# Two transformer blocks on one Trainium2 core: elementwise work moved off GpSimd, one PSUM division, zero-padded GLA queries, means taken earlier

## The chip, the core and the metric

The program runs on one core of a Trainium2 chip, in one launch. A core has a matrix engine (TensorE, called PE in the rows; its weight loads are listed apart as PEld), a vector engine (DVE), a scalar engine (ACT), GpSimd (POOL) and SyncE (SP), which issues the transfers from memory. TensorE reads operands from the on-chip SBUF and writes into PSUM, which has eight banks of 128 partitions by 512 floats. DVE and ACT read PSUM and SBUF; GpSimd works here on SBUF alone. The metric is device microseconds (us) for one execution.

## The reference, cut to what matters

Two blocks run one after the other on 512 tokens of width 1024 (the first with 16 extra "meta" tokens). All of it is in fp32.

```
first_block:   h += 0.5 * swiglu(rmsnorm(h))
               q,k,v,u,g_attn,g_ssm = split(rmsnorm(h) @ w_in)
               attn = sliding_window_attention(q,k,v)     # 16 heads of 64, blocks of 128, sink softmax
               y    = gelu(s5_ssm(u))                     # diagonal complex scan over time
               h   += (sigmoid(g_attn)*attn + sigmoid(g_ssm)*glu(y)) @ w_out
               h   += 0.5 * swiglu(rmsnorm(h)) ; return rmsnorm(h)
second_block, two layers i:
               m = mla_mixer(x) if i == 0 else gla_mixer(x)   # MLA: 16 heads with rope; GLA below
               x = layer_norm(sqrt(2)*x + m)                  # ln1
               x = layer_norm(sqrt(2)*x + conv_ffn(x))        # ln2
               x = x + sigmoid(x @ w_gate + b) * (p[i] @ w_proj)
gla_mixer, 4 heads, chunks n of 64 tokens:
               state = state * decay[n] + k_dec[n]^T v[n] ;  o[n] = q[n] @ state
               o = normalise(o) per head ; o * silu(r) @ w_o
```

## The kernel before, in words

Activations lie transposed: the residual is eight tiles `h` (`hr` without the meta tokens) of 128 features by the tokens. A projection (`proj`, `mm3`, L176) takes each fp32 weight tile of 128x1024, which `fetch` (L138) splits into a high part on ACT (`whi`, L86) and a low part on DVE (`wlo`, L66), and each operand likewise (`zh`, `zl`, or `mh`, `ml`), and adds the three products hi*hi, lo*hi, hi*lo in one PSUM bank. `nat` (L192) does the same with tokens on the output's partitions, 256 columns at a time. Both use the fp32r type, where a matmul is one record in the trace; a plain fp32 matmul is two records ("x2" in a row is one matmul).

The stages: swiglu of the first block; a projection stage; attention of the first block with four quarters of the state-space model woven in (`scores1` L717, `turn1`, `values1`, `ssm_quarter` L540); gates and output (`m3`), second swiglu; the MLA layer (`project`, `scores`, `turn`, `values`, `output`, L1171 to L1260); its two layer norms and convolution FFN (`conv_ffn` L981); the GLA layer (`recur` L1369); its two norms and FFN. A scheduler orders each engine's instructions when the program is built, from its own estimates; each engine then runs its queue strictly in that order, so an instruction that waits holds all that is queued behind it.

What the change touches:

- `pss` (L98) gives a PSUM bank under a tag, `banks` (L102) closes the pool of banks and opens another. Before, the division changes between b=6, s=2 (FFNs) and others for attention, MLA (L1262) and GLA (L1424).
- `sumsq` (L228) adds squares for an rms norm on GpSimd, except the last add.
- `ssm_quarter`: `t0` to `t3` (tiles `sq`, 128x528) are rotated by the tables `ct`, `st` (tile `tab`), scanned along time (L580, L581) and rotated back; of the eight full-width elementwise operations three are on DVE and five on GpSimd. Their results are the operands of the matmuls at L592 and L593.
- `scores1`: for each pair of heads the second head's probabilities (`sc`, times `dn` in tile `at`) are scaled on GpSimd in one operation.
- `Norm` (L886) is a layer norm. `centre` (L894) takes a mean over the first feature tile with a matmul by `oness` (L897) and subtracts it from all eight tiles before squares are summed. `put(k, m)` (L901) adds the mixer's or FFN's output tile `m` to `x`, and sums `x` (`ad`) and its square (`acc`, squares `nq`), the latter on GpSimd for k<5. `sums` (L924) reduces both on TensorE (L928), `factors` makes rsqrt, `bcast` (L240) spreads it by transposes (L244), `apply` (L942) scales, shifts and splits the eight tiles for the next projections.
- For ln1 of layer 0 the mean is taken in `mixer` (L1288), after the third group of MLA's output projection and ahead of the fourth; for ln1 of layer 1 in `put(0)`, with the first output tile.
- `rotate` (L1105) is rope: `x` is read from PSUM by one DVE multiplication over 128 partitions and four over 32.
- `recur` (L1369) runs GLA's recurrence. Per chunk one matmul (L1377) makes the update, DVE updates the state `S` (L83), and L1388 multiplies the queries `gq` of 64 tokens with the state: a stationary operand of 64 columns, into one half of a bank's partitions.

## Time and profile before

| | |
|---|---|
| three runs | 2620.64 us median (2620.52 to 2621.66) |
| profiled execution | 2621.09 us, span of the core 2619.3 us |
| TensorE busy | 2580.6 us, 99% of the span |
| TensorE's mean granted clock | 0.995 of full (2.4 GHz) |
| DVE, ACT, POOL busy | 1589.7, 962.0, 232.2 us |

A row of the timeline gives start, duration, engine, source line, operation, output<-inputs, shape and count, and in brackets the idle time just before it with what ended it. A matmul's modelled duration overlaps the next one's, so what one costs is read from start to start.

### The profile page before, as it was taken

How to read it: one execution, taken by the hardware profiler on the slowest of the kernel's cores; microseconds unless marked ns; L12 is line 12 of the kernel's file. 1: busy time of each engine (PE TensorE's matmuls, PEld its weight loads, DVE VectorE, ACT ScalarE, POOL GpSimd, SP SyncE). 2: the span in 40 equal slices, each digit the busy share in tenths (PEclk: the TensorE clock that was granted, in tenths of full speed). 3: DMA queues.
4: the chain of work that ended last, by engine and by line, in shares of the span. 5: the costliest groups of instructions: out<-in, count | busy, mean ns of one | idle time of the engine just before them, and what ended most of it. 6: DMA issues, size and time to landing. Idle time of an engine off the chain costs nothing.

```text
span 2619.3 us, 35036 instructions
## 1 busy us (share of the span) xinstructions
PE 2580.6 (99%) x13918; PEld 2188.3 (84%) x13918; DVE 1589.7 (61%) x2794; ACT 962.0 (37%) x1490; POOL 232.2 (9%) x190
## 2 busy tenths in 40 slices
PE   8999999999999999999999999999999999999999
PEld 8999999766888888887888878888878778888887
DVE  7985444685557544468776775555663356755556
ACT  4222223344333222234444454333353233433333
POOL 1000002231010000010000110000300011100030
PEclk9999999999999999999999999999999999999999
DMA  5443324332333333322112223333232222333332
GB/s 173 132 137 108 97 89 132 103 86 68 102 100 93 98 97 98 98 90 69 53 57 69 66 79 105 97 97 97 80 99 61 76 66 64 121 98 97 97 96 73
DMA packets 87749, 243.32 MB, mean 93 GB/s; under 512 B 20081, under 2 KB 26097, under 8 KB 87458
## 3 DMA queue, kind: packets, MB, share of 16 engines
q1 hardware_dynamic: 87586, 241.08, 30.2%
q8 instruction: 110, 1.80, 0.3%
q14 instruction: 53, 0.43, 0.1%
HBM read 229.11 MB, written 11.93 MB: 92 GB/s over the span
## 4 chain that ended last, share of the span: by engine, by line
PE 93%; DVE 4%; issue 1%; ACT 1%; DMA 0%; SPq 0%; POOL 0%; DVEq 0%; POOLq 0%; ACTq 0%
PE ps_b L176 62%; PE mm L176 16%; PE ps_b L192 6%; PE ps_o L1252 1%; PE ps_q L1224 1%; PE ps_o L1388 1%; PE ps_t L1240 1%; PE ps_u L1377 1%; DVE wlo L66 0%; PE ps_o L782 0%; DVE h L66 0%; DVE sq L66 0%; PE ps_q L1222 0%; PE ps_q L728 0%; PE ps_q L1223 0%
## 5 line engine op out<-in xcount | busy, mean ns | idle before, releaser
L86 ACT ACTIVATE whi<-raw 128x1024 fp32r<-128x1024 f32 (+2 forms) x418 | 432.6, 1038 | 1016.1 <-PE ps_b L176 664.1
L66 DVE TENSOR_TENSOR wlo<-raw,whi 128x1024 fp32r<-128x1024 f32 (+2 forms) x418 | 516.3, 1237 | 332.4 <-ACT whi L86 329.7
L176 PE MATMUL ps_b<-zh,whi 128*128 128x512 f32 (+1 forms) x1656 | 649.5, 393 | 6.9 <-ACT zh L86 2.4
L176 PE MATMUL ps_b<-zh,wlo 128*128 128x512 f32 (+1 forms) x1656 | 643.1, 389 | 0.0
L176 PE MATMUL ps_b<-zl,whi 128*128 128x512 f32 (+1 forms) x1656 | 638.8, 389 | 0.0
L176 PEld LDWEIGHTS ps_b<-zh,whi 128*128 128x128 f32 (+1 forms) x1656 | 310.7, 188 | 78.5 <-ACT zh L86 4.1
L176 PEld LDWEIGHTS ps_b<-zl,whi 128*128 128x128 f32 (+1 forms) x1656 | 310.8, 188 | 67.7 <-issue 2.6
L176 PEld LDWEIGHTS ps_b<-zh,wlo 128*128 128x128 f32 (+1 forms) x1656 | 310.7, 188 | 65.3 <-issue 0.8
L176 PE MATMUL ps_b<-mh,wlo 128*128 128x512 f32 x528 | 206.2, 391 | 0.0
L176 PE MATMUL ps_b<-ml,whi 128*128 128x512 f32 x528 | 205.4, 389 | 0.0
L176 PE MATMUL ps_b<-mh,whi 128*128 128x512 f32 x528 | 205.4, 389 | 0.0
L176 PE MATMUL mm<-zh,whi 128*128 128x264 f32 x800 | 163.1, 285 | 5.7 <-ACT whi L86 5.7
L176 PE MATMUL mm<-zl,whi 128*128 128x264 f32 x800 | 163.3, 285 | 1.7 <-DVE zl L83 1.7
L176 PE MATMUL mm<-zh,wlo 128*128 128x264 f32 x800 | 162.4, 284 | 0.0
L83 DVE SCALAR_TENSOR_TENSOR cv<-ps_b,vec,cv 128x511 f32<-128x511 f32 (+1 forms) x176 | 130.4, 745 | 15.1 <-ACT cv L86 13.7
L66 DVE TENSOR_TENSOR h<-h,ps_b 128x512 f32<-128x512 f32 x109 | 74.7, 686 | 97.5 <-PE ps_b L176 97.2
L176 PEld LDWEIGHTS mm<-zh,whi 128*128 128x128 f32 x800 | 125.0, 190 | 5.8 <-ACT whi L86 5.7
L176 PEld LDWEIGHTS mm<-zl,whi 128*128 128x128 f32 x800 | 125.1, 190 | 2.4 <-DVE zl L83 2.2
L176 PEld LDWEIGHTS mm<-zh,wlo 128*128 128x128 f32 x800 | 124.9, 190 | 0.0
L66 POOL TENSOR_TENSOR acc<-acc,sq 128x512 f32<-128x512 f32 (+1 forms) x26 | 39.2, 1507 | 937.3 <-ACT sq L86 899.2
L176 PEld LDWEIGHTS ps_b<-mh,whi 128*128 128x128 f32 x528 | 99.1, 188 | 21.1 <-issue 0.5
L176 PEld LDWEIGHTS ps_b<-mh,wlo 128*128 128x128 f32 x528 | 99.1, 188 | 21.0 <-issue 0.5
(426 smaller groups left out, 4015.1 us busy)
## 6 DMA issues: line engine op xcount, KB each, us to landing
raw<-in_ffn_w_dram SPq DMA_DIRECT2D x130, 512.0 KB, 3.5
raw<-in_w_up_dram SPq DMA_DIRECT2D x88, 512.0 KB, 3.7
raw<-in_w_down_dram SPq DMA_DIRECT2D x44, 512.0 KB, 3.6
raw<-in_w_in_dram SPq DMA_DIRECT2D x32, 512.0 KB, 3.6
raw<-in_mla_o_dram SPq DMA_DIRECT2D x16, 512.0 KB, 3.6
raw<-in_ple_g_dram SPq DMA_DIRECT2D x16, 512.0 KB, 3.7
raw<-in_glu_dram SPq DMA_DIRECT2D x8, 512.0 KB, 3.6
raw<-in_w_out_dram SPq DMA_DIRECT2D x8, 512.0 KB, 3.5
```

The lines of the kernel that those rows point to most:

```text
L66: return (e or V).tensor_tensor(o, a, b, op=op)
L83: return V.scalar_tensor_tensor(o, a, s, b, op0=op0, op1=op1)
L86: return SC.activation(o, a, f, **kw)
L176: last["pe"] = PE.matmul(o[:, i, :c1 - c0], lhs, x[k][r][:, c0:c1], start=(k == 0 and j == 0), stop=(k == kt - 1 and j == 2))
L192: PE.matmul(o[:m, :n], x[k][a][:, t0:t0 + m], w[b][:, kk_ * c + m0:kk_ * c + m0 + n], start=(k == 0 and i == 0), stop=(k == kt - 1 and i = ...
L1224: PE.matmul(p[:, :N], d["q"][e][:, bs], d["k"][e][:, :N], start=False, stop=True)
L1240: PE.transpose(pt[:, kt * P:(kt + 1) * P], sc[:, kt * P:(kt + 1) * P], ident)
L1252: PE.matmul(po[:, b * P:(b + 1) * P], vt[:, kt, e * P:(e + 1) * P], pT[:, kt * P:(kt + 1) * P], start=(kt == 0), stop=(kt == b))
L1377: PE.matmul(pu[c][:, :256], ek[b][rows, hc], vt[hh][rows, b])
L1388: PE.matmul(po[hh][-1][64 * c:64 * c + 64, (b % 2) * 256:(b % 2) * 256 + 256], qt[hh][:, n * 64:(n + 1) * 64], s_)
```

## The change

Six edits stand in one diff. One PSUM division (b, q and t with two banks, o and s with one) is kept from the end of attention on; `pss` takes the tags b, q, t in turn where b was asked for, and s, o for s; in MLA the tags are taken by name, and in GLA u means q, and o means o, s, t in turn. In the state-space quarters, in `sumsq` (except one call) and in `Norm`, operations that were on GpSimd are on DVE. The second head's scaling in `scores1` is four ACT operations. `centre` is a function of its own: for ln1 it is called during the third group of MLA's output (`gi == 2`) and during the second head of GLA's recurrence (`hh == 1`), and `put` only adds. In `rotate` ACT copies the swapped quarters out of PSUM and DVE works on 128 partitions. GLA's queries stand in a tile with zeros in the other chunk's 64 columns, so that L1388 (L1395 after) has 128 stationary columns and the two chunks add into all 128 partitions.

```diff
@@ -96,6 +96,10 @@
     def pss(tag="b"):
+
+        if tag in turns:
+            turns[tag].append(turns[tag].pop(0))
+            tag = turns[tag][-1]
         tag = tag if tag in psp["tags"] else "b" if "b" in psp["tags"] else "s"
@@ -108,6 +112,8 @@
     woff = {}
+    turns = {}
+    wide = dict(b=["b", "q", "t"], s=["s", "o"])
     zw, aw = 640, T1
@@ -225,7 +231,7 @@
-    def sumsq(tiles):
+    def sumsq(tiles, e=None):
         acc = zp.tile([P, aw], F32, name="acc")
@@ -234,7 +240,7 @@
                 act(sq[:, :n], t, AF.Square)
-                add(acc[:, :n], acc[:, :n], sq[:, :n], None if k == len(tiles) - 1 else GP)
+                add(acc[:, :n], acc[:, :n], sq[:, :n], None if k == len(tiles) - 1 else e)
         return acc[:, :n]
@@ -574,17 +580,17 @@
             mul(t3[:, sl], re, st[:, sl])
-        add(t0, t0, t1, GP)
-        sub(t2, t2, t3, GP)
+        add(t0, t0, t1)
+        sub(t2, t2, t3)
         fl = lambda t: t.rearrange("p a m -> p (a m)")
...
         mul(t0, t1, ct)
-        mul(t2, t1, st, GP)
+        mul(t2, t1, st)
         mul(t1, t3, st)
-        mul(t3, t3, ct, GP)
+        mul(t3, t3, ct)
         sub(t0, t0, t1)
-        add(t2, t2, t3, GP)
+        add(t2, t2, t3)
         py = pss()
@@ -744,7 +750,11 @@
                     mul(mt[:, :, 32 * s_:32 * s_ + NM], t[:, :, :NM], dn.unsqueeze(2).to_broadcast([P, 4, NM]))
-                    mul(t[:, :, NM:W], t[:, :, NM:W], dn.unsqueeze(2).to_broadcast([P, 4, W - NM]), GP if s_ else None)
+                    if s_:
+                        for i in range(4):
+                            act(t[:, i, NM:W], t[:, i, NM:W], AF.Copy, scale=dn[:, i:i + 1])
+                    else:
+                        mul(t[:, :, NM:W], t[:, :, NM:W], dn.unsqueeze(2).to_broadcast([P, 4, W - NM]))
                 live[u] = sc, mt
@@ -800,7 +810,8 @@
                     values1(units[ui - 1])
-        banks(b=6, s=2)
+        banks(b=2, q=2, t=2, o=1, s=1)
+        turns.update(wide)
         with tc.tile_pool(name="m3", bufs=2) as gp_:
@@ -883,43 +894,32 @@
+    def centre(x, a=1.0):
+
+        pc = pss("s")
+        PE.matmul(pc, oness, x)
+        c = zp.tile([P, aw], F32, name="R")[:, :S]
+        act(c, pc, AF.Copy, scale=a)
+        return c
+
     class Norm:
...
-        def __init__(self, pool, xs, a):
-            self.p, self.xs, self.a = pool, xs, a
+        def __init__(self, pool, xs):
+            self.p, self.xs = pool, xs
             self.aq = zp.tile([P, aw], F32, name="acc")[:, :S]
...
-        def centre(self):
...
         def put(self, k, m):
             x = self.xs[k]
+            add(x, x, m)
             if k == 0:
-                if self.a == 1.0:
-                    add(x, x, m)
-                else:
-                    stt(x, x, self.a, m, ALU.mult, ALU.add)
-                    self.centre()
-                    sub(x, x, self.c)
-                    for t in self.xs[3:]:
-                        stt(t, t, self.a, self.c, ALU.mult, ALU.subtract)
                 act(self.aq, x, AF.Square)
                 return
-            if self.a != 1.0 and k < 3:
-                stt(x, x, self.a, m, ALU.mult, ALU.add)
-                sub(x, x, self.c)
-            else:
-                add(x, x, m)
             sq = self.p.tile([P, S], F32, name="nq", bufs=3)
...
             add(self.ad, self.ad if k > 1 else self.xs[0], x)
-            add(self.aq, self.aq, sq, GP if k < 5 else None)
+            add(self.aq, self.aq, sq)
@@ -951,7 +951,7 @@
                 else:
-                    ts(xs[k], xs[k], gk, bk, e=GP)
+                    ts(xs[k], xs[k], gk, bk)
                 return chain(lambda: sub(z[k][1], xs[k], z[k][0].bitcast(F32)), prev)
@@ -978,7 +978,7 @@
-    def conv_ffn(li, xs, a, mixer):
+    def conv_ffn(li, xs, mixer):
@@ -1011,10 +1011,10 @@
-            norm = Norm(ph, xs, a)
+            norm = Norm(ph, xs)
             mixer(norm)
             z = close(norm, "ln1", "w_up")
-            norm = Norm(ph, xs, 1.0)
+            norm = Norm(ph, xs)
@@ -1038,6 +1038,7 @@
             def down(si, mids):
+                nonlocal cen
                 nt = 8 // len(mids)
@@ -1052,10 +1053,10 @@
                             if k == 0:
-                                norm.centre()
-                            sub(xs[k], xs[k], norm.c, GP)
-
-            j, pend = 0, None
+                                cen = centre(xs[0])
+                            sub(xs[k], xs[k], cen)
+
+            j, pend, cen = 0, None, None
             for si, seg in enumerate(SEGS):
@@ -1104,11 +1105,13 @@
-            mul(o, x, cosT)
+            xs = mp.tile([P, S], F32, name="xs", bufs=1)
             for i in range(4):
                 a, b = slice(32 * i, 32 * i + 32), slice(32 * (i ^ 1), 32 * (i ^ 1) + 32)
-                mul(t[a], x[b], sinT[b])
-            last["rot"] = add(o, o, t)
+                act(xs[a], x[b], AF.Copy)
+            mul(o, x, cosT)
+            mul(t, xs, sinT)
+            sub(o, o, t)
@@ -1134,7 +1137,7 @@
         oq = operand(cq, "mla_q_norm", "oq")
-        acc = sumsq(cq)
+        acc = sumsq(cq, GP)
         scale = 192.0 ** -0.5
@@ -1208,6 +1211,9 @@
                         add(hr[k], hr[k], p)
+                    if gi == 2:
+                        cen = centre(hr[0]) if k == 0 else cen
+                        sub(hr[k], hr[k], cen)
                     yield
@@ -1259,7 +1265,7 @@
         take([project(0)], 99)
-        banks(b=2, q=2, t=2, o=1, s=1)
+        turns.clear()
         units = [(hd_, b) for hd_ in range(16) for b in range(4)]
@@ -1283,15 +1289,12 @@
         take(oq_, 99)
-        banks(b=6, s=2)
+        turns.update(wide)
     rpc.__exit__(None, None, None)
     def mixer(norm):
-        norm.centre()
-        for k, x in enumerate(hr):
-            sub(x, x, norm.c, GP if k % 2 else None)
         take([output(3, norm.put)], 99)
-    conv_ffn(0, hr, 1.0, mixer)
+    conv_ffn(0, hr, mixer)
@@ -1344,8 +1347,12 @@
         def queries(i):
-            t = qt[i] = mp.tile([P, S], F32, name=f"gq{i}", bufs=1)
-            act(t, proj(wload("gla_q", 1024), P, 0, z, CS)[:, 0], AF.Copy, scale=128.0 ** -0.5)
+
+            t = qt[i] = mp.tile([P, 4, 2, P], F32, name=f"gq{i}", bufs=1)
+            v = proj(wload("gla_q", 1024), P, 0, z, CS)[:, 0].rearrange("p (b c t) -> p b c t", b=4, c=2)
+            for c in range(2):
+                GP.memset(t[:, :, c, 64 - 64 * c:128 - 64 * c], 0.0)
+                act(t[:, :, c, 64 * c:64 * c + 64], v[:, :, c], AF.Copy, scale=128.0 ** -0.5)
             yield
@@ -1385,8 +1392,8 @@
                     prev = s_
-                    PE.matmul(po[hh][-1][64 * c:64 * c + 64, (b % 2) * 256:(b % 2) * 256 + 256],
-                              qt[hh][:, n * 64:(n + 1) * 64], s_)
+                    PE.matmul(po[hh][-1][:, (b % 2) * 256:(b % 2) * 256 + 256], qt[hh][:, b, c], s_,
+                              start=(c == 0), stop=(c == 1))
                     yield
@@ -1421,11 +1428,15 @@
         take([queries(0), values(0), queries(1), keys(0)], 99)
-        banks(b=2, u=2, o=3, t=1)
+        turns.clear()
+        turns.update(u=["q"], o=["o", "s", "t"])
         for hh, fill in enumerate(([values(1), gates(0)], [keys(1), values(2), queries(2)],
...
                 take(fill, 1)
+                if hh == 1 and n < KD:
+                    cen = centre(hr[0], RT2) if n == 0 else cen
+                    stt(hr[n], hr[n], RT2, cen, ALU.mult, ALU.subtract)
             take(fill, 99)
@@ -1460,11 +1471,12 @@
                 norm.put(k, early[k][1])
-        banks(b=6, s=2)
+        turns.clear()
+        turns.update(wide)
         for k in range(2, 8):
...
-    conv_ffn(1, hr, RT2, mixer)
+    conv_ffn(1, hr, mixer)
     dump(hr, S)
```

Three places in the program, before and after. First TensorE's queue in GLA, in the first head's recurrence, where matmuls of L192 (L198 after) project values and gates between the recurrence's matmuls. Before:

```order
L192 MATMUL ps_b<-wlo,zh_16718 128x256
L1388 MATMUL ps_o<-S,gq_16828 64x256
L192 MATMUL ps_b<-whi,zh_16722 128x256
L192 MATMUL ps_b<-whi,zl_16723 128x256
L192 MATMUL ps_b<-wlo,zh_16722 128x256
L1388 MATMUL ps_o<-S,gq_16828 64x256
L192 MATMUL ps_b<-whi,zh_16694 128x256
```

Now, at the like place:

```order
L198 MATMUL ps_b<-wlo,zh_16748 128x256
L1395 MATMUL ps_o<-S,gq_16862 128x256
L198 MATMUL ps_b<-whi,zh_16752 128x256
L198 MATMUL ps_b<-whi,zl_16753 128x256
L198 MATMUL ps_b<-wlo,zh_16752 128x256
L198 MATMUL ps_b<-whi,zh_16756 128x256
L198 MATMUL ps_b<-whi,zl_16757 128x256
L198 MATMUL ps_b<-wlo,zh_16756 128x256
L1395 MATMUL ps_o<-S,gq_16862 128x256
L198 MATMUL ps_b<-whi,zh_16728 128x256
```

The number of matmuls is the same; the output's partitions are 128 where they were 64. Of the 32 matmuls of L1388, 27 follow one of L192 and 27 precede one; of those of L1395, 25 do. L1395 stands next to an update matmul of L1384 (L1377 before) six times on either side, where it was four.

Second DVE's queue in the first state-space quarter, around the two scans (L580 and L581; L586 and L587 after; the scan is listed as SCALAR_TENSOR_TENSOR), with the softmax operations of the first unit (tiles `at`, `mt`, `sc`) between. Before:

```order
L79 TENSOR_SCALAR at_5403<-at_5401 128x4
L580 SCALAR_TENSOR_TENSOR sq_5481<-tab,sq_5480 128x528
L66 TENSOR_TENSOR at_5398<-sink,at_5398 128x4
L66 TENSOR_TENSOR at_5401<-sink,at_5401 128x4
L66 TENSOR_TENSOR sq_5480<-sq_5481,tab 128x528
L581 SCALAR_TENSOR_TENSOR sq_5483<-tab,sq_5482 128x528
L66 TENSOR_TENSOR at_5399<-at_5399,at_5398 128x4
```

and now:

```order
L66 TENSOR_TENSOR sq_5483<-sq_5483,sq_5484 128x528
L66 TENSOR_TENSOR sq_5485<-sq_5485,sq_5486 128x528
L66 TENSOR_TENSOR at_5398<-at_5398,sink 128x4
L66 TENSOR_TENSOR at_5401<-at_5401,sink 128x4
L586 SCALAR_TENSOR_TENSOR sq_5484<-tab,sq_5483 128x528
L587 SCALAR_TENSOR_TENSOR sq_5486<-tab,sq_5485 128x528
L79 TENSOR_SCALAR at_5400<-at_5398 128x4
L79 TENSOR_SCALAR at_5403<-at_5401 128x4
L66 TENSOR_TENSOR sq_5483<-sq_5484,tab 128x528
L66 TENSOR_TENSOR sq_5485<-sq_5484,tab 128x528
```

GpSimd's queue loses the five operations of the quarter and the scaling of `sc`; before it held them in this order:

```order
L66 TENSOR_TENSOR sq_5480<-sq_5480,sq_5481 128x528
L66 TENSOR_TENSOR sq_5482<-sq_5482,sq_5483 128x528
L66 TENSOR_TENSOR sq_5482<-sq_5481,tab 128x528
L66 TENSOR_TENSOR sq_5483<-sq_5483,tab 128x528
L66 TENSOR_TENSOR sc<-sc,at_5402 128x4x128
L66 TENSOR_TENSOR sq_5482<-sq_5482,sq_5483 128x528
```

Third TensorE's queue at the end of GLA: L1446 is the output projection of the first two tiles, L897 the mean of ln1, L176 the third output tile. Before:

```order
L1446 MATMUL ps_b<-zh_18601,wlo 128x512
L1446 MATMUL ps_b<-zl_18602,whi 128x512
L1446 MATMUL ps_b<-zh_18601,wlo 128x512
L897 MATMUL ps_b<-h_72,oness 128x512
L176 MATMUL ps_b<-zh_17801,whi 128x512
```

The mean's matmul (L900 after) now stands in the second head's recurrence, among the projections of L198:

```order
L198 MATMUL ps_b<-wlo,zh_16732 128x256
L198 MATMUL ps_b<-whi,zh_16736 128x256
L198 MATMUL ps_b<-whi,zl_16737 128x256
L900 MATMUL ps_s<-h_72,oness 128x512
L198 MATMUL ps_b<-wlo,zh_16736 128x256
L198 MATMUL ps_b<-whi,zh_16740 128x256
```

What came directly ahead of the third output tile is gone from there.

## Rows read from the trace of the kernel before

**Rows 1.** TensorE's waits over the whole span: us in total, times, longest us.
```profile
PE ps_b L592 <- DVE sq L66: 3.0, 1, 3.0
...
PE ps_b L928 <- DVE ad L66: 2.8, 1, 2.8
...
PE mm L176 <- DVE zl L83: 1.7, 1, 1.7
...
PE ps_b L176 <- DVE q L66: 1.7, 1, 1.7
...
PE ps_s L897 <- DVE zl L66: 1.4, 1, 1.4
...
PE ps_u L1377 <- DVE ek L66: 1.3, 1, 1.3
...
PE ps_b L897 <- DVE h L83: 1.1, 1, 1.1
```

**Rows 2.** Timeline of TensorE in the GLA recurrence, 2078.3 to 2079.4.
```profile
2078.36 0.28 PE L192 MATMUL ps_b<-wlo,zh 128*128 128x256 f32 x1
2078.56 0.65 PE L1388 MATMUL ps_o<-S,gq 128*64 128x256 f32 x2
...
2079.36 0.28 PE L192 MATMUL ps_b<-whi,zl 128*128 128x256 f32 x1
```

**Rows 3.** Timeline of TensorE in MLA attention, 1229.8 to 1230.4.
```profile
1229.85 0.28 PE L1223 MATMUL ps_q<-kl,qr 128*128 128x256 f32 x1
1229.97 0.59 PE L1224 MATMUL ps_q<-kn,qn 128*128 128x256 f32 x2
1230.40 0.27 PE L1240 MATMUL ps_t<-ident,sc 128*128 128x128 f32 x1
```

**Rows 4.** Weight loads by form, GLA stage and MLA stage: count, busy, mean ns.
```profile
L1388 PEld LDWEIGHTS ps_o<-S,gq 128*64 128x64 f32 x64 | 6.1, 134 | 5.3 <-issue 1.3 <-DVE ek L66 0.3
...
L1224 PEld LDWEIGHTS ps_q<-kn,qn 128*128 128x128 f32 x128 | 21.5, 189 | 1.1
```

**Rows 5.** Timeline of TensorE at layer 0's two norms, ln1 then ln2.
```profile
1512.93 1.87 PE L928 MATMUL ps_b<-onesd,ad 128*128 128x1 f32 x8 [2.78 <-DVE ad L66]
...
1522.87 0.48 PE L176 MATMUL ps_b<-pth,whi 128*128 128x512 f32 x1
...
1887.14 1.05 PE L928 MATMUL ps_b<-onesd,ad 128*128 128x1 f32 x8
...
1892.60 0.47 PE L176 MATMUL ps_b<-pth,whi 128*128 128x512 f32 x1
```

**Rows 6.** Windows: us, then busy and count of PE, PEld, DVE, ACT, POOL, clock, DMA.
```profile
484.00:600.00 116.00, 104.57 (x506) 73.20 (x506) 100.67 (x274) 49.47 (x160) 41.50 (x35) 0.97 0.32 88
...
1512.00:1523.00 11.00, 10.07 (x37) 8.81 (x38) 3.78 (x16) 2.48 (x5) 0.00 (x0) 0.53 0.01 1
...
2150.00:2162.00 12.00, 9.76 (x34) 6.58 (x33) 9.01 (x14) 5.41 (x8) 0.00 (x0) 0.86 0.37 117
```

**Rows 7.** Timeline of POOL and DVE in the state-space quarters.
```profile
518.76 1.89 POOL L66 TENSOR_TENSOR sc<-sc,at 128x1024 f32<-128x1024 f32 x1 [12.43 <-issue]
...
518.88 1.80 DVE L66 TENSOR_TENSOR at<-at,sink 128x4 f32<-128x4 f32 x1
...
520.94 0.21 DVE L66 TENSOR_TENSOR mt<-sc,at 128x64 f32<-128x64 f32 x1
```

**Rows 8.** Groups by form over the span, DVE and ACT: count, busy, mean ns.
```profile
L66 DVE TENSOR_TENSOR sq<-sq,sq 128x528 f32<-128x528 f32 x4 | 5.9, 1470 | 0.0
...
L66 DVE TENSOR_TENSOR sq<-sq,tab 128x528 f32<-128x528 f32 x8 | 5.6, 702 | 0.9 <-POOL sq L66 0.8
...
L66 DVE TENSOR_TENSOR mt<-sc,at 128x64 f32<-128x64 f32 x16 | 11.0, 690 | 0.5
...
L86 ACT ACTIVATE pTm<-ps_t 64x512 f32<-64x512 f32 x8 | 4.7, 583 | 15.0 <-PE ps_t L756 15.0
```

**Rows 9.** Timeline of DVE in the scaling after ln2 of layer 0.
```profile
1895.16 0.54 DVE L80 TENSOR_SCALAR h<-h,vec 128x512 f32<-128x512 f32 x1
```

4 lines of the change are left out of this document (removed).

## The prediction

> **What bounds the kernel now.** I read the page first: TensorE is busy for 99% of the span, so nothing that another engine does faster is worth anything unless TensorE waits for it, or unless TensorE's own time changes. The reader is to see three kinds of lost time on TensorE, each in another view.
>
> The first kind is plain waits. The list of TensorE's waits [rows 1] is short, and nearly all end on DVE: the state-space sums before L592 (3.0 us), the sum before the norm's reduction L928 (2.8), the operands at the start (1.7), the rope operations (1.7), the two means L897 (1.4 and 1.1), the keys before the first GLA update (1.3).
>
> The second kind is matmuls issued further apart than their columns need, which counts as busy and shows only from start to start in the timeline. In MLA [rows 3] an fp32r matmul of 256 columns (L1223) is followed after 0.12 us by L1224, which is plain fp32 with the same 256 columns and 128 stationary ones, and after 0.43 more by the next. In GLA [rows 2] L1388, plain fp32 with 256 columns too, but 64 stationary ones, starts 0.20 after the L192 ahead of it, and from that L192 at 2078.36 to the second one after L1388, at 2079.36, is 1.00 us; two L192 of 0.12 taken off, one L1388 costs 0.76. So 0.33 us of each L1388 is not columns.
>
> The third kind is the clock. After the wait of 2.8 us, from 1512 to 1523, the granted clock is 0.53 [rows 6], so TensorE runs at the lower of its two levels (1.2 GHz, not 2.4). The same reductions, embeddings and transposes take 9.94 us at ln1 of layer 0 (1512.93 to 1522.87) and 5.46 at ln2 (1887.14 to 1892.60) [rows 5]: 4.5 us are the clock's. Around the mean of ln1 in layer 1 the mean granted clock over 12 us is 0.86 [rows 6], which is 1.7 us of clock lost.
>
> The sum below is made against the profiled execution's 2621.1 us; the median of the runs is 0.45 lower.
>
> **Zeros in GLA.** The columns streamed stay the same, the stationary side doubles. 25 of the 32 matmuls stand between 128-wide ones on both sides of the queue and should cost 0.43 instead of 0.76: 25 x 0.33 = 8.3 us. Six stand next to an update matmul (64 rows), which stays as it is; I give those half, 1 us. So 9.3, taken as **9**. The upper end is all 32 at 0.33, 10.6. The lower end comes from the weight loads: one of 64 columns takes 134 ns and one of 128 takes 189 [rows 4], and if the 55 ns were not hidden, 64 loads would take back 3.5 us, leaving 5.5. L1224's 0.43 has loads of 189 in it and shows none, so I take the full gain. The two half-width ACT copies and two GpSimd memsets per head that fill the new tile are made while projections keep TensorE busy; uncovered, they would cost the first head about 1 us once.
>
> The Trainium skill ("TensorE: Matmul & The Clock Gate", LDWEIGHTS) speaks against this edit: a load takes its columns over 1.2 GHz, so 53 ns more for 128 than for 64. By that, if nothing hid it, 64 loads would give 3.4 us back, and the sum below would be 3.4 us worse; the measured loads differ by 55 ns, and the row of L1224 shows them hidden.
>
> **Norm of layer 0, ln1.** The mean's wait (1.4) goes, since the mean is taken a projection group earlier, with eight DVE subtractions spread over that group, and PE's matmul for it now stands among score and value matmuls. The wait of 2.8 for the last sum goes if DVE is less behind. Before the sums DVE had four subtractions and waited for GpSimd's; now it has four more additions of squares (about 0.7 each) and no subtractions. At ln2, where DVE has as much to do per output tile, the wait was a fraction of a microsecond and the clock stayed up [rows 5]. Without the wait the 4.5 us of clock go as well. All of it is 8.7; I take **7.5**, since a small wait like ln2's will stay. The lower end is 1.4, if DVE still ends late.
>
> **Norm of layer 1, ln1.** The mean and five scalings move into the second head's recurrence, where TensorE has projections queued behind the mean's matmul and DVE's own work in the recurrence is one operation per chunk. The 1.1 us wait and the 1.7 of clock go, with a little for ACT's copy of the mean: **3**, between 1.1 and 3.5.
>
> **State-space quarters and attention.** From 484 to 600 us TensorE idles 116 - 104.57 = 11.4 us, its clock is at 0.97 (3.4 us lost), DVE is busy for 100.67 and GpSimd for 41.50 [rows 6]. The change puts 20 operations on DVE at 0.70 each [rows 8]: 14.1 us. But DVE loses time while GpSimd works: an operation on 128x4 took 1.80 us under a GpSimd operation of 1.89 [rows 7]; the 528-wide one that stands beside GpSimd's averages 1.47 against 0.70; the 16 `mt` average 0.69 [rows 8] against 0.21 alone [rows 7]. The last two alone are 4 x 0.77 + 16 x 0.48 = 10.8 us that DVE gets back, and the many 128x4 operations some more. So DVE's load hardly changes, and a chain with five GpSimd links gets shorter links. The 32 scalings on ACT have room (ACT is busy 49 of 116). I take **5** of the 11.4 + 3.4; the bounds are all of it, 14.8, and a loss of 3.3 if only the 10.8 come back.
>
> The Trainium skill ("SBUF — State Buffer", SBUF: two separate sides) says that DVE and GpSimd share one pair of ports as a lock: whoever comes second waits for the whole instruction. The 1.80 beside 1.89 agrees. By that rule alone all of GpSimd's time in SBUF would come back to DVE, and this part would end near its upper end; I don't count on it, since DVE also has its own work then.
>
> **PSUM and rope.** With one division the first MLA projections need not wait for the old pool, and rope frees its bank after one DVE operation and four ACT copies of some 0.58 us each [rows 8] in place of five DVE operations. The wait of 1.7 goes: **1.5**, between 0 and 1.7. ACT gets 36 copies, 21 us spread over the layer, while TensorE works on other units; uncovered, a burst of four would hold a transposed tile back for 2.3 us. GLA's first update no longer waits for the whole pool: **1** of 1.3.
>
> **Start.** Squares added on DVE rather than beside it: **1** of the 1.7 us wait, at least 0.
>
> **What is paid.** In each of four norms three scalings of 0.54 us [rows 9] come onto DVE, between operations that TensorE's first projections follow closely. I take 0.4 us each, **1.5** in all, at most 5. Everything else (subtractions in the down projections, squares in the other norms) lies under dense projections.
>
> Sum: 9 + 7.5 + 3 + 5 + 1.5 + 1 + 1 - 1.5 = 26.5. 2621.1 - 26.5 = 2594.6, less 0.45: **2594 us**.
>
> **The rivals.** (1) *DVE's waits only move.* What GpSimd gave up makes DVE late again in the quarters and at ln1 of layer 0, so that both give nothing beyond the mean's wait: 9 + 1.4 + 3 + 1.5 + 1 + 1 - 1.5 = 15.4, or **2605**. For it speaks that DVE is busy for 87% of 484 to 600; against it the contention, and that ln2 has no such wait. Chance 0.18. (2) *The wide weights are not free.* GLA gives 5.5 (**2598**) or nothing (**2603**). For it speak the loads, 55 ns longer; against it L1224. Chance 0.08. (3) *DVE becomes the bound*, and the kernel is slower: the operations beside GpSimd don't get shorter, and the new work lies on the path whole: 14.1 in the quarters and, in four norms, four additions at 0.7 and three scalings at 0.54, 4.4 each, 17.7 in all. Against that stand 9 + 1.4 + 3 + 1.5 + 1 + 1 = 16.9: 14.9 slower, **2636**. It decides as soon as more than 16.9 of the 31.8 us lie on the path. The 1.80 us operation speaks against it. Chance 0.04.
>
> **How the numbers follow.** My forecast has 0.70, its own range 2583 to 2602. The range that takes in rivals 1 and 2 but not the far ends is 2583 to 2607; rival 3 and a share of 1 lie above, all waits gone (about 2580) below. A change of 0.2% is 5 us, about what this measurement can tell. Faster has my forecast, rivals 1 and 2, less a little for sums that miss: 0.94; same 0.02; slower 0.04.
>
> **What would show it.** In the changed profile: L1395 followed by the next matmul 0.43 us after its start, with no gap of 0.20 ahead of it; no wait of L900; at ln1 of layer 0 the stretch from L928 to the transposes at 5.5 us and the clock at 1.00; no small DVE operation above 1 us between 484 and 600, and TensorE's idle time there about 5 us less; no wait on rope. The prediction is wrong if L1395 still costs 0.7, or if a wait of 2 us or more on DVE's sums or on the state-space operands comes back and takes the clock down with it.

## The result and the profile after

The changed kernel takes 2593.18 us (median of 4 runs, 2590.1 to 2594.72), the kernel before 2620.58 on the same chip: a ratio of 0.9895, 95% interval 0.9878 to 0.9913. Run again on another occasion it gave 0.9897 (0.9882 to 0.9912). The prediction was 2594.

TensorE's waits in the changed kernel, the longest after the first weight; columns as in [rows 1]:

```profile
PE ps_b L576 <- DVE sq L66: 2.5, 3, 1.2
PE ps_b L182 <- ACT vt L86: 1.9, 1, 1.9
PE ps_b L576 <- DMA M<-k_d: 1.6, 1, 1.6
PE ps_b L598 <- DVE sq L66: 1.6, 2, 1.3
...
PE ps_t L928 <- DVE ad L66: 0.6, 1, 0.6
```

Of the seven waits of [rows 1] none stands here as it was. The 3.0 us before the state-space sums is 1.6 in two pieces, the 2.8 before L928 is 0.6, those at the start, at the two means and before the first GLA update are gone. So is the wait on rope. Others are new or longer: 2.5 us and 1.6 (this one for a transfer) at the quarters' first matmuls (L576), and 1.9 us on ScalarE's copies of v, where the kernel before waited 1.0:

```profile
PE ps_b L176 <- ACT vt L86: 1.0, 1, 1.0
```

TensorE's timeline around one L1395, and at the two norms where the clock fell:

```profile
1988.22 0.28 PE L198 MATMUL ps_b<-wlo,zh 128*128 128x256 f32 x1
1988.34 0.59 PE L1395 MATMUL ps_o<-S,gq 128*128 128x256 f32 x2
1988.58 0.47 PE L198 MATMUL ps_b<-whi,zh 128*128 128x256 f32 x1
1988.88 0.28 PE L198 MATMUL ps_b<-whi,zl 128*128 128x256 f32 x1
...
1497.35 1.05 PE L928 MATMUL ps_t<-onesd,ad 128*128 128x1 f32 x8 [0.63 <-DVE ad L66]
...
1500.17 0.63 PE L182 MATMUL ps_b<-ptl,whi 128*128 128x512 f32 x1
1500.59 0.63 PE L182 MATMUL ps_b<-pth,wlo 128*128 128x512 f32 x1
...
1504.86 0.92 PE L250 MATMUL ps_o<-ident,rs_y 128*128 128x128 f32 x4
...
2533.56 1.05 PE L928 MATMUL ps_q<-onesd,ad 128*128 128x1 f32 x8
...
2536.40 0.63 PE L182 MATMUL ps_t<-ptl,whi 128*128 128x512 f32 x1
```

From the L198 at 1988.22 to the second one behind L1395, at 1988.88, is 0.66 us, where [rows 2] had 1.00. At ln1 of layer 0 matmuls of 512 columns are 0.42 apart (1500.17 to 1500.59), so the clock is still low there after a wait of only 0.63. At ln2 of layer 1 it is low too, and no wait stands ahead of L928 there.

Two windows, columns as in [rows 6]:

```profile
484.00:600.00 116.00, 109.37 (x549) 78.61 (x551) 95.32 (x294) 62.21 (x191) 3.47 (x9) 1.00 0.32 93
1495.00:1506.00 11.00, 10.37 (x45) 8.49 (x43) 4.84 (x18) 2.54 (x5) 0.00 (x0) 0.69 0.01 1
```

TensorE idles 6.6 us between 484 and 600, where it was 11.4, and DVE is busy for less (95.3 against 100.7), though it has 20 operations more. The cause is in DVE's groups by form from 470 to 640 us, three of the changed kernel and then one of the kernel before:

```profile
L66 DVE TENSOR_TENSOR sq<-sq,sq 128x528 f32<-128x528 f32 x16 | 10.9, 701 | 0.0
...
L66 DVE TENSOR_TENSOR mt<-sc,at 128x64 f32<-128x64 f32 x16 | 3.5, 221 | 0.6
...
L66 DVE TENSOR_TENSOR at<-at,sink 128x4 f32<-128x4 f32 x16 | 2.4, 158 | 0.0
```

```profile
L66 DVE TENSOR_TENSOR at<-at,sink 128x4 f32<-128x4 f32 x16 | 5.8, 380 | 0.0
```

The `mt` take 0.22 us and not 0.69, the full-width additions 0.70 and not 1.47 [rows 8], the small `at` 0.16 and not 0.38.

For the sums by stage I cut each profile at six marks that every version has: the first reduction of a sum of squares (L253, L259 after), and the first transpose by `bcast` (L244, L250 after) at MLA's start and at each layer norm. Durations in us between marks:

| profile | start | to MLA's start | MLA and ln1 | FFN and ln2 | GLA and ln1 | FFN and ln2 | span |
|---|---|---|---|---|---|---|---|
| before | 24.3 | 1174.0 | 323.3 | 370.2 | 306.3 | 369.7 | 2619.3 |
| changed | 19.9 | 1168.7 | 316.2 | 370.1 | 293.4 | 371.4 | 2591.3 |
| changed, second profile | 19.9 | 1169.9 | 311.8 | 371.3 | 293.4 | 369.8 | 2587.5 |
| e1 narrow queries | 19.9 | 1168.3 | 313.3 | 371.3 | 300.4 | 369.8 | 2594.5 |
| e2 quarters on GpSimd | 20.4 | 1173.4 | 313.3 | 371.4 | 293.3 | 369.8 | 2593.2 |
| e3 scaling on GpSimd | 20.1 | 1170.8 | 311.8 | 369.8 | 291.6 | 370.1 | 2585.7 |
| e4 squares on GpSimd | 24.2 | 1170.9 | 313.4 | 371.3 | 293.4 | 369.8 | 2594.5 |
| e5 norms on GpSimd | 19.8 | 1168.8 | 316.2 | 369.7 | 291.3 | 370.2 | 2587.6 |
| e6 late means | 19.7 | 1169.1 | 319.4 | 369.9 | 289.6 | 371.3 | 2590.6 |
| e7 old banks and rope | 20.4 | 1171.7 | 318.5 | 371.4 | 296.6 | 369.8 | 2599.9 |
| e8 padded keys | 20.8 | 1171.5 | 311.7 | 371.2 | 286.6 | 370.0 | 2583.4 |
| e9 old rope | 19.9 | 1170.8 | 323.8 | 369.9 | 290.3 | 371.4 | 2597.6 |
| e10 banks alone | 24.5 | 1175.4 | 321.0 | 369.7 | 299.7 | 371.2 | 2613.1 |

The last 51.5 us are alike in all. The FFN columns show a step of about 1.6: that is one fall of the clock to its lower level (below), which lasts 3.4 us and so costs up to 1.7. So a single column is good to a fall or two, unless one looks up in the granted clock where the falls stand. The ratios below, with intervals of about 0.0014 either way (3.7 us), are the wider yardstick.

Two things have to be taken off before the columns are read. The GLA column holds three falls in the kernel before, two in each profile of the changed kernel, one in e1, none in e6 and e9; less 1.7 for each fall the changed kernel's is 290.0, and those of e6 and e9 are 289.6 and 290.3 as they stand. And the mark at MLA's start is not at the same place in the work: between the first transpose of the second swiglu's norm and this mark, where TensorE hardly idles in either, the changed kernel has 1744 matmuls in 392.2 us, the kernel before 1730 in 390.0. So 2.2 us of the changed kernel's gain are missing in the second column and too many in the third.

### The profile page after: what moved, and what is told of

Its sections match the earlier page's. It is cut to its first block, busy times and chain, and to the rows that moved or that the text cites. A ratio compares the mean times of both kernels' runs of the same rounds, so it can differ in the third digit from the quotient of the medians.

```text
span 2591.3 us, 35009 instructions
## 1 busy us (share of the span) xinstructions
PE 2566.1 (99%) x13918; PEld 2188.1 (84%) x13918; DVE 1573.6 (61%) x2859; ACT 995.3 (38%) x1562; POOL 84.9 (3%) x98
## 4 chain that ended last, share of the span: by engine, by line
PE 96%; DVE 2%; issue 0%; SPq 0%; ACT 0%; DMA 0%; DVEq 0%
PE ps_b L182 27%; PE ps_q L182 19%; PE ps_t L182 18%; PE mm L182 16%; PE ps_b L198 5%; PE ps_o L1258 1%; PE ps_q L1230 1%; PE ps_o L792 1%; PE ps_q L734 1%; PE ps_t L1246 1%; PE ps_q L1384 1%; DVE sq L66 1%; PE ps_b L1457 0%; PE ps_t L198 0%; PE ps_t L776 0%
## 5 line engine op out<-in xcount | busy, mean ns | idle before, releaser
L182 PE MATMUL ps_b<-zh,whi 128*128 128x512 f32 (+1 forms) x692 | 272.8, 394 | 2.9 <-DVE sq L66 0.9
L182 PE MATMUL ps_b<-zl,whi 128*128 128x512 f32 (+1 forms) x692 | 269.8, 390 | 0.0
L182 PE MATMUL ps_b<-zh,wlo 128*128 128x512 f32 (+1 forms) x692 | 269.6, 390 | 0.0
L182 PE MATMUL ps_q<-zh,whi 128*128 128x512 f32 (+1 forms) x488 | 189.3, 388 | 1.2 <-ACT zh L86 1.2
L182 PE MATMUL ps_q<-zl,whi 128*128 128x512 f32 (+1 forms) x488 | 189.4, 388 | 0.0
L182 PE MATMUL ps_q<-zh,wlo 128*128 128x512 f32 (+1 forms) x488 | 189.2, 388 | 0.0
L182 PE MATMUL ps_t<-zh,whi 128*128 128x512 f32 x476 | 185.6, 390 | 0.6 <-ACT zh L86 0.6
L182 PE MATMUL ps_t<-zl,whi 128*128 128x512 f32 x476 | 185.6, 390 | 0.0
L182 PE MATMUL ps_t<-zh,wlo 128*128 128x512 f32 x476 | 185.2, 389 | 0.0
L182 PEld LDWEIGHTS ps_b<-zh,whi 128*128 128x128 f32 (+1 forms) x692 | 129.2, 187 | 33.6 <-issue 2.8
L182 PEld LDWEIGHTS ps_q<-zh,whi 128*128 128x128 f32 x488 | 91.6, 188 | 20.8 <-ACT zh L86 2.1
L182 PEld LDWEIGHTS ps_q<-zl,whi 128*128 128x128 f32 x488 | 91.6, 188 | 20.4 <-DVE zl L66 1.3
```

The source lines that it names most:

```text
L182: last["pe"] = PE.matmul(o[:, i, :c1 - c0], lhs, x[k][r][:, c0:c1], start=(k == 0 and j == 0), stop=(k == kt - 1 and j == 2))
```

## The experiments

Each is the changed kernel with one group of edits taken back or added, except e10, which starts from the kernel before. The ratio is to the kernel before.

| run | median us | ratio | 95% interval |
|---|---|---|---|
| changed, again | 2590.7 | 0.9897 | 0.9882 to 0.9912 |
| e1 narrow queries | 2598.8 | 0.9923 | 0.9910 to 0.9935 |
| e2 quarters on GpSimd | 2595.1 | 0.9908 | 0.9894 to 0.9921 |
| e3 scaling on GpSimd | 2593.1 | 0.9895 | 0.9881 to 0.9908 |
| e4 squares on GpSimd | 2597.8 | 0.9917 | 0.9903 to 0.9931 |
| e5 norms on GpSimd | 2594.9 | 0.9905 | 0.9890 to 0.9921 |
| e6 late means | 2596.0 | 0.9908 | 0.9894 to 0.9921 |
| e7 old banks and rope | 2601.7 | 0.9927 | 0.9915 to 0.9940 |
| e8 padded keys | 2586.1 | 0.9866 | 0.9853 to 0.9880 |
| e9 old rope | 2599.5 | 0.9919 | 0.9905 to 0.9932 |
| e10 banks alone | 2617.4 | 0.9987 | 0.9978 to 0.9995 |

**The changed kernel again.** No edit.

> The changed kernel once more, unaltered, for a second profile beside the ones below. Two accounts of why the clock fell from 2536.2 to 2539.6 us in the first profile of it (ln2 of layer 1), where TensorE's rows up to there are those of the kernel before, which kept the clock. If the fall is chance (which stretches get the lower level differs from one execution to the next with the same instructions), this profile has another set of falls, and its span differs from 2591.3 by multiples of about 1.7 us, the price of one fall of 3.4 us. If the fall belongs to the changed order, it stands at the same place again. The ratio to the kernel before is 0.9895 either way, within 0.1%.

TensorE's timeline at the same norm of the second profile:

```profile
2531.37 1.05 PE L928 MATMUL ps_q<-onesd,ad 128*128 128x1 f32 x8
...
2535.31 0.39 PE L182 MATMUL ps_b<-pth,whi 128*128 128x512 f32 x1
2535.53 0.39 PE L182 MATMUL ps_b<-ptl,whi 128*128 128x512 f32 x1
...
2535.99 0.60 PE L250 MATMUL ps_o<-ident,rs_y 128*128 128x128 f32 x4
```

No fall here, from the same instructions at the same distances; and at ln1 of layer 0, behind the same wait of 0.63, L928 to L250 is 4.62 us (1496.90 to 1501.52) where the first profile took 7.51. Its falls are others: apart from the last 4 us it has four of 3.4 us each, at 504, 1870, 1945 and 1965 us, the first profile six, at 1198, 1499 (two in a row), 1963 (two in a row) and 2536. So the fall at ln2 of layer 1 does not belong to the changed order. Which stretches lose the clock differs from one execution to the next, a fall costs about 1.6 us, and the span (2587.5) is two falls shorter.

**e1, narrow queries.**

```diff
-                    PE.matmul(po[hh][-1][:, (b % 2) * 256:(b % 2) * 256 + 256], qt[hh][:, b, c], s_,
-                              start=(c == 0), stop=(c == 1))
+                    PE.matmul(po[hh][-1][64 * c:64 * c + 64, (b % 2) * 256:(b % 2) * 256 + 256],
+                              qt[hh][:, n * 64:(n + 1) * 64], s_)
```

> The changed kernel with GLA's queries 64 columns wide again, nothing else undone. My account: a matmul with 64 columns between two of 128 costs 0.34 us more than its columns, and the changed kernel has some 24 such turns fewer, so this run is 24 x 0.34 = 8.1 us slower than the changed kernel (about 2601), and L1395's neighbours stand 1.00 us apart as in the kernel before. Rival: the recurrence got shorter by the PSUM banks taken in turn and the longer weight loads (55 ns each, 64 of them, 3.5 us) take part of it back; then this run is at most 4.6 us slower, 0 if the banks did it all.

TensorE's timeline around one such matmul of this run:

```profile
1986.18 0.28 PE L198 MATMUL ps_b<-wlo,zh 128*128 128x256 f32 x1
1986.39 0.65 PE L1392 MATMUL ps_o<-S,gq 128*64 128x256 f32 x2
1986.97 0.39 PE L198 MATMUL ps_b<-whi,zh 128*128 128x256 f32 x1
1987.19 0.28 PE L198 MATMUL ps_b<-whi,zl 128*128 128x256 f32 x1
```

1.01 us again, and GLA's stage is 7.0 longer. But its profile has one fall of the clock in this stage, at 1945 us, where the changed kernel's have two. The same window of this run and then of the second profile of the changed kernel, columns as in [rows 6]:

```profile
1963.00:1970.00 7.00, 7.00 (x60) 7.00 (x61) 0.84 (x2) 0.20 (x1) 0.00 (x0) 1.00 0.00 0
```

```profile
1963.00:1970.00 7.00, 7.00 (x48) 7.00 (x48) 0.84 (x2) 0.20 (x1) 0.00 (x0) 0.76 0.00 0
```

With 1.7 us for the fall that is missing here, the narrow queries cost 8.7. The timeline gives the same from start to start. In both programs 21 of the 32 matmuls stand between 128-wide ones on both sides; each costs 0.78 here (the columns of its neighbours taken off) and 0.44 in the changed kernel, 7.1 us in all. Ten stand beside one update matmul and cost 0.14 more here, 1.4 in all; the last, between two updates, gains nothing. That is 8.5 us. The account holds; the rival, at most 4.6 us, does not, and its loads of 55 ns do not show. By the ratios the run is 0.0026 slower (6.8 us), with intervals that just overlap.

**e2 and e3, the two halves of what left GpSimd in attention.**

```diff
-        add(t0, t0, t1)
-        sub(t2, t2, t3)
+        add(t0, t0, t1, GP)
+        sub(t2, t2, t3, GP)
```

and likewise the quarter's two products and its last sum (e2); and, apart from that (e3):

```diff
-                    if s_:
-                        for i in range(4):
-                            act(t[:, i, NM:W], t[:, i, NM:W], AF.Copy, scale=dn[:, i:i + 1])
-                    else:
-                        mul(t[:, :, NM:W], t[:, :, NM:W], dn.unsqueeze(2).to_broadcast([P, 4, W - NM]))
+                    mul(t[:, :, NM:W], t[:, :, NM:W], dn.unsqueeze(2).to_broadcast([P, 4, W - NM]), GP if s_ else None)
```

> The changed kernel with the five operations of each state-space quarter back on GpSimd; the second head's scaling stays on ScalarE. Account A (contention: DVE is held up whenever GpSimd works): 20 GpSimd operations of about 1.5 us overlap DVE again, the full-width additions on DVE go from 0.70 back towards 1.4 us, TensorE's idle time between 475 and 625 us grows by about half of the 7.5 us that it lost, and the run is 3 to 5 us slower than the changed kernel. Account B (the chain of a quarter with links on two engines is what made the matmuls of L598 late): the wait of L598 on the sums comes back at 2 to 3 us in at least one quarter, with the small operations on DVE still short; also 3 to 5 us, but the waits and not the durations carry it. If neither matters, and the scaling was all, 0 to 1 us.

> The changed kernel with the second head's scaling back on GpSimd, one operation of 128x1024 per unit; the quarters stay on DVE. Account A (contention): the operations that run beside it are the small ones of the softmax, so the sixteen operations on mt go from 0.22 back to about 0.69 us and those on 128x4 from 0.16 to 0.28 and more, 13 us of DVE time in all; TensorE waits 2 to 5 us more in 475 to 640 and the run is 2 to 5 us slower than the changed kernel. Rival: DVE has slack there, and the scaling's place makes no difference to TensorE: within 1 us.

DVE's groups by form from 470 to 640 us, of e2 and then of e3:

```profile
L66 DVE TENSOR_TENSOR mt<-sc,at 128x64 f32<-128x64 f32 x16 | 7.0, 435 | 0.4
...
L66 DVE TENSOR_TENSOR at<-at,sink 128x4 f32<-128x4 f32 x16 | 5.5, 356 | 0.0
```

```profile
L66 DVE TENSOR_TENSOR mt<-sc,at 128x64 f32<-128x64 f32 x16 | 11.4, 715 | 0.4
...
L66 DVE TENSOR_TENSOR at<-at,sink 128x4 f32<-128x4 f32 x16 | 2.4, 166 | 0.0
```

The slowing beside GpSimd comes back, and differs with the partner: the quarter's operations hold up `at` (0.36 from 0.16) and partly `mt` (0.43 from 0.22), the scaling holds up `mt` alone (0.72). My expectation for e3 had `at` slow as well; it isn't. What TensorE feels of it stands in its waits, here those of e2 from 470 to 640 us:

```profile
PE ps_b L598 <- DVE sq L66: 5.5, 4, 3.0
```

In e2 the wait of 3.0 on the state-space sums is back, and the second column is 3.5 to 4.7 us longer than in the two profiles of the changed kernel; in e3 it is 1.0 to 2.1. Falls do not explain it: e2 has one before MLA's start, e3 none (granted clock 1.00 from 418.7 to 798.8), the changed kernel none in its first profile and one in its second. Net of them e2 is 3.0 to 3.6 us longer and e3 2.1 to 2.7, so both halves count, the quarters somewhat more. In e2 durations (A) and the chain (B) return together, and it doesn't part them; in e3 no wait on the sums is above 1.3 us, as in the changed kernel, so there it is durations. By the ratios alone neither run is told from the changed kernel.

**e4, the rms norms' squares on GpSimd.**

```diff
-    def sumsq(tiles, e=None):
+    def sumsq(tiles, e=GP):
```

> The changed kernel with the additions of squares for the rms norms back on GpSimd, the layer norms untouched. In the changed kernel TensorE has no wait of 1.7 us at 9 us, and its matmuls of 264 columns stand 0.12 apart from 10.4 us on, where it was 17.3 before. My account: the wait came from GpSimd's additions beside DVE, and it also held the clock at 1.2 GHz for 5 us more; then here the wait of 1.5 to 2 us is back between 9 and 12 us, the clock rises at about 17 us, and the run is 4 to 4.5 us slower than the changed kernel, all of it in the first 25 us. Rival: the start varies by itself, as falls elsewhere do; then the rise stays at 10 to 11 us and the run is 0 to 1 us slower.

TensorE's timeline at the start:

```profile
10.99 0.51 PE L182 MATMUL mm<-zl,whi 128*128 128x264 f32 x2 [1.74 <-DVE zl L83]
...
13.45 0.65 PE L182 MATMUL mm<-zh,whi 128*128 128x264 f32 x2
13.89 0.65 PE L182 MATMUL mm<-zl,whi 128*128 128x264 f32 x2
...
16.29 0.28 PE L182 MATMUL mm<-zh,whi 128*128 128x264 f32 x1
16.41 0.41 PE L182 MATMUL mm<-zl,whi 128*128 128x264 f32 x2
```

The 1.74 is back, two matmuls take 0.44 (13.45 to 13.89) until 16.3, the granted clock is 0.51 from 12.8 to 16.2, and the start is 4.3 us longer, as my account had it. In the kernel before the matmuls have the same pace until 17.2, but its granted clock reads 1.00 there; that it was the lower level is inferred from the pace.

**e5, the layer norms on GpSimd.**

```diff
-            add(self.aq, self.aq, sq)
+            add(self.aq, self.aq, sq, GP if k < 5 else None)
```

and likewise the three scalings and ln2's subtractions.

> The changed kernel with the layer norms' additions of squares (k below 5), three scalings and the subtractions of ln2's mean back on GpSimd; the means stay early. Account A (contention): DVE's operations beside GpSimd's get long again (ad above 1 us, wlo above 2 us, as before), DVE ends late at ln1 of layer 0, TensorE waits 2 us or more at L928 and the clock falls for the whole chain; 3 to 6 us slower than the changed kernel. Account B (GpSimd took work from a DVE that is behind): the wait of 0.63 us at L928 goes, and the run is up to 1 us faster. In between, if the early mean alone made the gain: within 1 us.

DVE's groups by form of this run, 1475 to 1500 us, and TensorE's wait:

```profile
L66 DVE TENSOR_TENSOR ad<-ad,h 128x512 f32<-128x512 f32 x6 | 5.3, 882 | 0.1
...
PE ps_t L928 <- DVE ad L66: 1.9, 1, 1.9
```

Account A by its mechanism (`ad` 0.69 in the changed kernel, the wait 0.6), at a smaller size: 1.3 us more of wait. The stage is as long as in the first profile of the changed kernel, but that one has a fall more (granted clock 0.50 from 1198.3 to 1201.6), so it is 1.4 longer net of falls. Account B is out. By time the run is not told from the changed kernel.

**e6, late means.**

```diff
-                    if gi == 2:
-                        cen = centre(hr[0]) if k == 0 else cen
-                        sub(hr[k], hr[k], cen)
...
     def mixer(norm):
+        cen = centre(hr[0])
+        for k, x in enumerate(hr):
+            sub(x, x, cen, GP if k % 2 else None)
```

and in layer 1 the mean and the scalings in `put`, as before.

> The changed kernel with both ln1 means taken where the kernel before took them (layer 0: after the third group, alternate subtractions on GpSimd; layer 1: with the first output tile). My account: TensorE waits again at the mean's matmul, 1.4 us in layer 0 and 1.1 us plus 0.7 us for the mean's copy in layer 1, with one more fall of 1.7 us in layer 1, and in layer 0 DVE has four subtractions more ahead of the sums (2.4 us), so that the wait at L928 is 2 us or more and the clock falls for 7 us (3.4 us lost): 3.5 + 6 = 9.5 us slower than the changed kernel. Rival: in layer 0 GpSimd's work in the norm, not the mean, made DVE late; then layer 0 gives only the mean's wait, and the run is 4 to 5 us slower.

TensorE's waits of this run:

```profile
PE ps_t L938 <- DVE ad L66: 4.2, 1, 4.2
```

Of TensorE's waits that line (L938 is L928 of this run) is the one that returns. At L928 layer 0 behaves as I said, and more, but no wait stands at its mean; layer 1 loses nothing: its stage is 289.6, and no wait stands at the mean. So the waits of 1.4 and 1.1 us at the means of [rows 1] are not the means'. The sum of 9.5 us was too high: by the ratios the run is 0.0011 slower (3 us), which is not told from the changed kernel. In layer 0 the late mean brings four subtractions on GpSimd with it, and the run does not part the two.

**e7, e9 and e10, the PSUM division and rope.** e7 has both as before, e9 rope alone; e10 is the kernel before with the new division alone. One of the division's four places as e7 has it (rope's edits are in the diff of the change):

```diff
-        turns.clear()
-        turns.update(u=["q"], o=["o", "s", "t"])
+        banks(b=2, u=2, o=3, t=1)
```

> The changed kernel with the four changes of the PSUM division and rope on DVE alone, as before. My account: TensorE waits again on rope (1.7 us at the first MLA projections) and on the keys before the first GLA update (1.3 us), and for nothing else: 2 to 3 us slower than the changed kernel. Rival: the banks taken in turn matter all through the FFNs and GLA, where a matmul group otherwise waits for its bank; then waits on evacuations appear in those stages and the run is over 4 us slower. Second rival: what the old pools cost is hidden, and the wait of 1.9 us that the changed kernel has at 1196 us (on the copies of v) is the same wait under another name; within 1 us.

> The changed kernel with rope alone as before (five DVE operations on the bank, no copies on ScalarE); the one PSUM division stays. The run with the old division and the old rope was 8 us slower than the changed kernel, where I had expected 2 to 3. If the division did it (each opening of a pool waits for the last reader of the old one), rope alone gives back only its own wait: the wait on rope of 1.7 us returns and the wait of 1.9 us on the copies of v goes, within 1 us of the changed kernel. If rope's copies are a part of the gain, 2 us or more slower.

> The kernel before with the one PSUM division alone: banks kept from the end of attention on and tags taken in turn; every operation stays on its engine, the means late, the queries narrow. If the waits of 1.4 and 1.1 us at the two ln1 means, and of 1.3 us before the first update, are the openings of a pool (they wait for the last reads of the old one), all three go here although the means stay where they are: 3.8 us, with the copy of layer 1's mean (0.7) perhaps, and one fall of the clock of 1.7 us in layer 1: 4 to 6 us faster than the kernel before. If they are the means' own waits, as the prediction took them, only 1.3 us goes: within 2 us of the kernel before.

TensorE's timeline of e7 at the end of MLA and of GLA, where a pool of banks opens:

```profile
1480.83 0.50 PE L182 MATMUL ps_b<-zh,whi 128*128 128x512 f32 x1 [1.41 <-DVE zl L66]
...
2139.49 0.50 PE L182 MATMUL ps_b<-zh,whi 128*128 128x512 f32 x1 [2.25 <-DVE h L66]
```

No mean stands here (both are early), but the waits of [rows 1] at L897 do, on the same tiles (`zl` and `h`), the second twice as long: the first matmul into the new pool waits for operations that read the old one's banks last. And e10, with late means, has neither; its window at the end of GLA, where [rows 6] had 9.76 of 12 and a clock of 0.86:

```profile
2135.00:2165.00 30.00, 30.00 (x145) 24.80 (x145) 17.63 (x34) 12.60 (x19) 1.14 (x2) 1.00 0.28 88
```

So the pools made these waits, as e10's first account says. Its time is 0.0013 of the kernel before's (3.4 us), less than that account's 4 to 6, with an interval that takes in both accounts; the waits decide. GLA's stage gains 6.6 us, 3.4 of it two falls fewer, but at ln1 of layer 0 the wait only moves. TensorE's waits there, e10, then e9:

```profile
PE ps_t L935 <- DVE ad L66: 4.2, 1, 4.2
```

```profile
PE ps_t L928 <- DVE ad L66: 4.0, 1, 4.0
PE ps_b L182 <- DVE qn L66: 2.2, 2, 2.0
PE ps_b L198 <- DVE q L66: 2.2, 1, 2.2
...
PE ps_b L182 <- DVE kn L66: 1.8, 1, 1.8
```

e9 was expected within 1 us of the changed kernel and is slower by 0.0022 of the time (5.8 us, by ratios); MLA's stage is the longest of all, with the clock at 0.50 from 1504.5 to 1514.5, around its wait at ln1. With the one division and the old rope, TensorE waits three times for about 2 us on DVE's operations behind the first MLA projections (`qn`, `q`, `kn`), and DVE, which in the changed kernel is 0.6 us late at ln1, is 4.0 late. In e7, with the old banks, no wait stands at L928. The new rope under the old banks was not run. My expectation for e7 (2 to 3 us) was too low: 0.0030 (7.9 us). The waits of 1.4, 2.2, 1.3 (before the first update) and 1.7 us (on rope) make 6.6 of it.

**e8, padded keys.** The idea of the queries applied to the updates: keys with zeros in the other chunk's rows.

```diff
-                    PE.matmul(pu[c][:, :256], ek[b][rows, hc], vt[hh][rows, b])
+                    PE.matmul(pu[c][:, :256], kz[b][:, c, hc], vt[hh][:, b])
...
-            t = qt[i] = mp.tile([P, 4, 2, P], F32, name=f"gq{i}", bufs=1)
+            t = qt[i] = mp.tile([P, 4, 2, P], F32, name="gq", bufs=2)
```

> The changed kernel, with GLA's keys too in a tile with zeros in the other chunk's rows (two DVE operations on 64 partitions in place of one on 128, four tiles of 128x1024 zeroed in part by GpSimd, the queries in two buffers in turn for the space), so that the 32 update matmuls of L1384 take 128 rows and not 64. If what costs 0.34 us is the turn between a 64-wide operand and a 128-wide one, and not the columns, then it goes here as well: 32 x 0.34 = 10.8 us, less half a microsecond for the longer evacuation of the keys before the first update: 9 to 10.8 us faster than the changed kernel, with L198, update and L198 as close as columns allow (0.12, 0.43). Rival: 64 rows are not what 64 columns are, and only the narrow side of the stationary operand costs; then within 1 us of the changed kernel.

This run is faster than both kernels: 0.9866, its interval below that of the changed kernel run again. GLA's stage is 6.8 us shorter with two falls, as many as in the changed kernel, the time 8 by ratios, not 9 to 10.8. My count was wrong, as two updates can share their turns. TensorE's timeline of the changed kernel, a single update and then two:

```profile
1976.39 0.70 PE L1384 MATMUL ps_q<-gv,ek 64*128 64x256 f32 x2
1977.02 0.39 PE L198 MATMUL ps_b<-whi,zh 128*128 128x256 f32 x1
...
1992.87 0.70 PE L1384 MATMUL ps_q<-gv,ek 64*128 64x256 f32 x4
1993.50 0.39 PE L198 MATMUL ps_b<-whi,zh 128*128 128x256 f32 x1
```

and of e8:

```profile
1982.20 0.59 PE L1394 MATMUL ps_q<-gv,kz 128*128 128x256 f32 x2
1982.63 0.59 PE L1405 MATMUL ps_o<-S,gq 128*128 128x256 f32 x2
```

One update takes 0.63 us, and two of them, on rows 0 to 63 and 64 to 127, take 0.63 together; on 128 rows one takes 0.43. With the 0.19 us more that the turn at their edges takes, a single one gains 0.39 by the zeros, a pair loses 0.04: 20 singles and 6 pairs make 7.6.

## Why the prediction was right, and where it was not

The total held: 28.0 us in the profile against a sum of 26.5. In part that is luck: the start and the quarters gave 6 us more than I had counted, the MLA layer 4 less, what I had set down as paid (1.5) did not come, and one more fall of the clock in the last FFN (1.7) did. Point by point:

- **Zeros in GLA, 9.** Mechanism right, size 8.5 (e1). I had misread the queue: 25 have a 128-wide matmul on one side, but only 21 on both; eleven and not six stand next to an update, and ten of them gave 0.14 each. The loads' 55 ns cost nothing, so rival 2 is out.
- **Norm of layer 0, 7.5.** L900 waits for nothing, and the wait for the last sum is 0.63. But the step that gave the 1.4 us to the mean was wrong: it was the opening of a pool (e7, e10). What the early mean, with its subtractions off GpSimd, does is keep DVE from being 4.2 us late (e6). The step "without the wait the 4.5 us of clock go" failed in the first profile (1495 to 1506: clock 0.69) and held in the second. Together with rope the stage gave 7.1 and 11.5 in the third column, so 4.9 and 9.3 with the mark put right, where I had 9; the clock, with as much lost as before in the first profile and nothing in the second, is the difference.
- **Norm of layer 1, 3.** The waits went, but for the pool's sake; late means cost nothing here (e6). The right size under the wrong edit.
- **GLA as a whole, 13** (9, 3 and 1): 12.9 in both profiles. Of it 6.9 are the turns: from start to start the recurrence's matmuls beyond their neighbours' columns cost 42.6 us before, 44.1 in e1 and 35.6 in the changed kernel, so the zeros give 8.5, and the changed order, in which six pairs of updates stand together and not nine, takes 1.6 back. Another 3.1 are the waits of 1.3, 1.1 and 0.7 (the copy of the mean) that are gone, 1.7 the clock (5.1 us lost before, 3.4 after); about 1 is left that I can't place.
- **Quarters and attention, 5:** 7.5 and 6.4 up to the second swiglu's norm (5.3 and 4.1 in the table's second column, where the mark hides 2.2). Of that 3.4 and 1.7 are what falls of the clock cost the kernel before there beyond the changed kernel. TensorE's idle time from 484 to 600 us is 4.8 us less, as the prediction had it. DVE got back more than the 10.8 us that I counted on: `mt` 7.5 (11.0 to 3.5) and the `at` rows besides.
- **Rope and PSUM, 1.5 and 1.** The wait on rope (1.7) went, and the one on ScalarE's copies of v grew from 1.0 to 1.9, so 0.8 is left of it. That is the case that I had named uncovered: four of rope's copies take 2.54 us on ScalarE (1194.78 to 1197.32), the copy of v comes behind them, and TensorE goes on at 1197.88. That the old rope under the new division costs some 6 us more (e9) I had not seen: the terms of the sum are not independent.
- **Start, 1.** This is the term that I sized worst: 4.4. I took the 1.7 us of wait and left out the clock, which by the pace of the matmuls stays low until 17.3 us with the wait; without it full speed begins at 10.4 (e4).
- **Paid, -1.5.** Nothing of it shows. The first FFN column, which holds the scalings of ln1 of layer 0, is 370.1 against 370.2 before, and with the scalings back on GpSimd (e5) it is 369.7.

Rival 1, that DVE's waits only move, did not come true in the changed kernel, but it is what e6, e9 and e10 do at ln1 of layer 0. In the changed kernel DVE works there from 1480.9 to 1497.9 with one pause of 0.2 us, and ends just 0.6 us late. How late DVE is without the early mean (4.2), with the norm's work on GpSimd (1.9) and with the old rope (4.0) was measured; that tiles of the last group, in banks taken in turn, all wait for the last head and reach DVE at once (their additions start at 1480.9, 1481.5 and 1482.1) is read from the timeline and was not tried by itself. Rival 3 is out: DVE is busy for 1573.6 us, less than the 1589.7 before.

## What to carry to other kernels

Look first at which DVE operations get long while GpSimd works: an operation that moves from GpSimd to DVE can cost DVE less than it frees there, so count both. Look at what opens and closes around a wait before giving it to the instruction that waits: two waits named after a mean were the price of opening a PSUM pool. And a wait early in the kernel, or ahead of a chain of small matmuls, is to be priced with the clock that it can take along. Before two profiles are compared stage by stage, look up the falls of the clock in each and take them off: here they hid a fifth of what the zeros gave.
